# Low halves of the mixer's weights: a negated copy on ScalarE and an accumulating DMA in place of VectorE's subtraction

## The chip, the core and the metric

The kernel runs on one core of a Trainium2 chip. The metric is the device time of one execution in microseconds: 2360.43 us is the median of three runs, which lie between 2358.93 and 2362.97 us.

## The reference

Two transformer-like blocks follow each other on 1024 tokens of width 1024, all in float32. What matters here is the first block's input projection and its two branches:

```python
h = rms_norm(x, g_mix[l])
z = jnp.einsum("bsd,de->bse", h, w_in[l]) + b_in[l]
va, ga, xb, gb, sa, sb = jnp.split(z, cuts, axis=-1)
u = va * jax.nn.sigmoid(ga)
u = causal_depthwise_conv(u, conv_a_w[l], conv_a_b[l])
...
v = causal_depthwise_conv(xb, conv_b_w[l], conv_b_b[l])
v = rg_lru(v, w_rg_a[l], b_rg_a[l], w_rg_x[l], b_rg_x[l], lam[l])
y_b = jnp.einsum("bsc,cd->bsd", v * jax.nn.gelu(gb), w_b_out[l])
m = jax.nn.sigmoid(sa) * y_a + jax.nn.sigmoid(sb) * y_b
```

`w_in` has 7168 columns, `rg_lru` holds two small matrices per head (16 heads of width 96) and a scan over time. An output projection, an MLP and the whole second block come after; the change does not touch their code.

## The kernel before, in words

Activations lie transposed: channels on the 128 partitions, tokens along the row, in two halves of 512 tokens. To keep float32 precision every operand of a matrix product is split into a high part in fp32r and the low part that is left, and a product is three matmuls: low by high, high by low, high by high. A weight unit is a tile of 128 by 1024: eight input chunks of one block of 128 output channels. One product of a unit with one half of the tokens (`ct`, L134) is therefore 24 matmuls of 512 columns, 16 on L124 and 8 on L127, into one PSUM bank; four banks (`pm`) rotate.

`weight` (L102 to L111) makes a unit ready: SP issues the load of 512 KB into a staging tile `wst` (L106; two such tiles), ScalarE copies it into the high part `wh` in fp32r (L108), and VectorE subtracts that from the staging tile into the low part `wl` (L110). There are four tiles each of `wh` and `wl` (`N_W`, L1241), so a new unit's copy waits until PE is done with an older one. The three instructions run under a raised priority (`W_AHEAD`), which places them ahead of the program's order in each engine's queue; each queue then runs in order.

`mixer_in` (L508) makes four rounds. A round r first runs `branch_b_in` (L370) for three units of the recurrent branch: two products, bias on ScalarE (L376), a first tap on ScalarE (L381), three taps on VectorE (L383), a split (L131, L132). Then comes the filler: in the rounds 0 to 2 `branch_a_pair` (L312), whose four units all stay loaded while the first half of the tokens passes and then the second; in round 3 two `sig_chunk`s. Then the gates: one unit `w_rg` (L399), and for each of four heads (n = 0 to 3) four small products, and a chain on ScalarE of sigmoid (L417), exp (L422), tanh (L426), square (L429), then VectorE (L430), then square root (L433); for n below 3 also a unit of the gelu gate (L437), two products and the gelu on ScalarE (L443, L444). VectorE multiplies and scans (L456 to L460). At the end of a round some `sig_chunk`s (L467): two products and a sigmoid on ScalarE (L473). The 31 taps of the other branch (`conv_a`, L358 to L365) fill VectorE's queue throughout, at a lowered priority.

ScalarE needs another function table for each kind of function. A change of table shows in the trace as idle time of 1.31 us ahead of an instruction.

Of the kernel before, what the change touches and what calls it, by code (L numbers as in the profile page):

```python
# [9 lines left out]
F32 = mybir.dt.float32  # L10
F32R = mybir.dt.float32r
AF = mybir.ActivationFunctionType
ALU = mybir.AluOpType
# [35 lines left out]
class Act:  # L49
    def __init__(self, n):  # L50
        self.n = n
        self.h = {}
        self.l = {}
# [8 lines left out]
class Builder:  # L62
    def __init__(self, nc, tc, io, out):
        self.nc, self.tc, self.io, self.out = nc, tc, io, out
        self.n = 0
        self.log1p = set()

    def name(self, s):
        self.n += 1
        return f"{s}_{self.n}"  # L70
# [31 lines left out]
    def weight(self, src, cols=1024):  # L102
        nc = self.nc
        with self.tc.high_priority(offset=W_AHEAD):
            st = self.wst.tile([P, cols], F32, tag="wst", name=self.name("wst"))
            nc.sync.dma_start(st, src)  # L106
            h = self.wh.tile([P, cols], F32R, tag="wh", name=self.name("wh"))
            nc.scalar.activation(h, st, AF.Copy)  # L108
            l = self.wl.tile([P, cols], F32R, tag="wl", name=self.name("wl"))
            nc.vector.tensor_tensor(l, st, h.bitcast(F32), ALU.subtract)  # L110
        return h, l  # L111

    def mm3(self, ps, terms, ordered=False):
# [393 lines left out]

    def mixer_in(self):  # L508
        self.uc = {}
        n_s = (0, 2, 5, 7, 12)  # L510
        for r in range(4):
            if r == 0:
                self.sig_chunk(0, (0,), self.w_sig)
                for c in range(2):
                    self.uc[c] = self.page(f"e{c}")
                    self.conv_a(c, self.a_first[c][2], self.uc[c])
            sig = list(range(max(n_s[r], 1), n_s[r + 1]))
            self.branch_b(r, lambda: [self.branch_a_pair(2 * r + 2)] if r < 3 else [self.sig_chunk(c) for c in sig[:2]])
            for c in (sig[2:] if r == 3 else sig):
                self.sig_chunk(c)  # L520
        self.u = Act(KC)
        for hf in range(2):
            self.ln_stats(hf)
        ws = [self.sig_chunk(12 + i, (0,)) for i in range(4)]
        self.ln_apply(0)
        for i in range(4):
            self.sig_chunk(12 + i, (1,), ws[i])
        self.ln_apply(1)
# [832 lines left out]
```

## Time and profile before

| | |
|---|---|
| median of 3 runs | 2360.43 us |
| the profiled execution, its own time | 2360.36 us |
| its span, first to last instruction | 2358.7 us |
| PE busy | 2309.5 us (98%), 10488 matmuls |
| VectorE (DVE) busy | 1707.4 us (72%) |
| ScalarE (ACT) busy | 896.0 us (38%) |
| GpSimd (POOL) busy | 18.8 us (1%) |
| mean granted TensorE clock | 0.992 of full speed |
| DMA | 199.48 MB, mean 85 GB/s |

The shares are means over a kernel whose stages differ. The four rounds of `mixer_in` lie between about 46 and 640 us. A busy PE in these pages is one whose matmuls overlap each other: the rate is read better from the number of matmuls in a stretch than from its busy time.

### The profile page before, as it was taken

The numbers are of one execution on the slowest core, as the hardware profiler recorded it, in microseconds if no ns is written. First come the engines' busy times: TensorE is split into PE (matmuls) and PEld (weight loads), VectorE is DVE, ScalarE is ACT, GpSimd is POOL, SyncE is SP. The second block draws the span as 40 slices with busy tenths as digits, with TensorE's granted clock in tenths as the row PEclk, the third lists the DMA queues.
The fourth block names the chain that finished last, engine by engine and source line by source line (L and its number), as shares of the span: only waits on it lengthen the run. The fifth ranks groups of instructions, "written<-read, shape, count | busy, mean of one in ns | idle before, by whom it ended". The sixth has DMA issues, their size and how long they took to land. (4 is left out here: it accounts for less than half of the span.)

```text
span 2358.7 us, 27111 instructions
## 1 busy us (share of the span) xinstructions
PE 2309.5 (98%) x10488; PEld 1903.8 (81%) x10488; DVE 1707.4 (72%) x2567; ACT 896.0 (38%) x1372; POOL 18.8 (1%) x44
## 2 busy tenths in 40 slices
PE   8999999999999999999999999999799999999998
PEld 6887888878878888888888888887687888888777
DVE  8999999895674334686676767678957467775866
ACT  6445463555552112342212212124624344443422
POOL 0000000000000000000000000000000000000000
PEclk9999999999999999999999999999899999999999
DMA  4223223233424323251211111111332111223422
GB/s 157 81 65 98 70 80 104 78 104 94 150 81 155 105 85 99 76 183 45 63 45 54 46 55 52 54 54 52 112 109 66 55 50 57 83 65 106 139 85 72
DMA packets 81090, 199.48 MB, mean 85 GB/s; under 512 B 9776, under 2 KB 12336, under 8 KB 80960
## 3 DMA queue, kind: packets, MB, share of 16 engines
q1 hardware_dynamic: 80960, 197.75, 26.5%
q8 instruction: 82, 1.34, 0.2%
q14 instruction: 48, 0.39, 0.1%
HBM read 157.83 MB, written 38.31 MB: 83 GB/s over the span
## 5 line engine op out<-in xcount | busy, mean ns | idle before, releaser
L124 PE MATMUL pm<-acth,wl 128*128 128x512 f32 (+1 forms) x2032 | 786.6, 389 | 9.9 <-ACT b L473 5.0
L124 PE MATMUL pm<-actl,wh 128*128 128x512 f32 (+1 forms) x2032 | 787.7, 389 | 0.4 <-DVE actl L132 0.4
L127 PE MATMUL pm<-acth,wh 128*128 128x512 f32 (+1 forms) x2032 | 510.2, 387 | 0.0
L124 PEld LDWEIGHTS pm<-acth,wl 128*128 128x128 f32 x2032 | 383.4, 189 | 89.7 <-ACT b L473 6.3
L124 PEld LDWEIGHTS pm<-actl,wh 128*128 128x128 f32 x2032 | 383.5, 189 | 79.7 <-DVE actl L132 2.4
L127 PEld LDWEIGHTS pm<-acth,wh 128*128 128x128 f32 x2032 | 377.6, 188 | 76.1 <-issue 0.7
L108 ACT ACTIVATE wh<-wst 128x1024 fp32r<-128x1024 f32 x181 | 190.7, 1056 | 336.8 <-PE pm L127 238.1
L110 DVE TENSOR_TENSOR wl<-wst,wh 128x1024 fp32r<-128x1024 f32 x181 | 220.7, 1222 | 110.5 <-ACT wh L108 109.6
L807 DVE TENSOR_TENSOR x<-pm,x 128x512 f32<-128x512 f32 x240 | 161.2, 689 | 66.4 <-PE pm L127 51.7
L124 PE MATMUL pm<-e,wh 128*128 128x512 f32 x480 | 186.9, 389 | 0.0
L124 PE MATMUL pm<-e,wl 128*128 128x512 f32 x480 | 178.5, 390 | 0.0
L668 ACT ACTIVATE wh<-wst 128x1024 fp32r<-128x1024 f32 (+1 forms) x56 | 53.4, 954 | 260.6 <-PE pm L127 225.1
L127 PE MATMUL pm<-e,wh 128*128 128x512 f32 x480 | 141.8, 390 | 0.0
L358 DVE SCALAR_TENSOR_TENSOR e<-roll,pv,e 128x507 f32<-128x507 f32 (+14 forms) x174 | 119.9, 741 | 0.0
L124 PEld LDWEIGHTS pm<-e,wh 128*128 128x128 f32 x480 | 90.2, 188 | 18.9
L127 PEld LDWEIGHTS pm<-e,wh 128*128 128x128 f32 x480 | 90.1, 188 | 18.9
L124 PEld LDWEIGHTS pm<-e,wl 128*128 128x128 f32 x480 | 90.3, 188 | 18.4
L692 PE MATMUL pa<-acth,wl 128*128 128x512 f32 x224 | 87.3, 390 | 0.0
L692 PE MATMUL pa<-actl,wh 128*128 128x512 f32 x224 | 87.3, 390 | 0.0
L119 PE MATMUL pm<-e,wh 128*128 128x512 f32 x256 | 80.4, 399 | 0.6 <-DVE e L275 0.6
L131 ACT ACTIVATE e<-b 128x512 fp32r<-128x512 f32 x64 | 40.3, 632 | 103.1 <-DVE b L799 97.6
L702 DVE TENSOR_TENSOR b<-b,pa 128x512 f32<-128x512 f32 x70 | 46.8, 685 | 37.1 <-PE pa L692 36.0
(365 smaller groups left out, 3181.8 us busy)
## 6 DMA issues: line engine op xcount, KB each, us to landing
wst<-in_w_in SPq DMA_DIRECT2D x89, 512.0 KB, 3.5
wst<-in_w SPq DMA_DIRECT2D x64, 512.0 KB, 3.5
sig<-b SPq DMA_DIRECT2D x32, 256.0 KB, 2.7
ld<-sig SPq DMA_DIRECT2D x32, 256.0 KB, 2.6
a<-p SPq DMA_DIRECT2D x24, 256.0 KB, 3.7
wst<-in_w_b_out SPq DMA_DIRECT2D x12, 512.0 KB, 4.6
y<-b SPq DMA_DIRECT2D x24, 256.0 KB, 2.3
wst<-in_w_out SPq DMA_DIRECT2D x12, 512.0 KB, 3.5
```

What stands on the lines that cost most here:

```text
L108: nc.scalar.activation(h, st, AF.Copy)
L110: nc.vector.tensor_tensor(l, st, h.bitcast(F32), ALU.subtract)
L119: self.nc.tensor.matmul(ps, a, b, start=i == 0, stop=i == n - 1)
L124: self.nc.tensor.matmul(ps, a, b, start=i == 0, stop=i == n - 1)
L127: self.nc.tensor.matmul(ps, aH, bH, start=i == 0, stop=i == n - 1)
L131: self.nc.scalar.activation(H, srcap, AF.Copy)
L358: ops.append(lambda k=k: V.scalar_tensor_tensor(out[:, k:], x[:, :HALF - k], taps[k], out[:, k:], ALU.mult, ALU.add))
L668: nc.scalar.activation(h[:, :n], src, AF.Copy)
L692: self.nc.tensor.matmul(ps, (aH, aL)[i], (bH, bL)[j], start=n == 0, stop=n == 11)
L702: V.tensor_tensor(out, a, b, op)
L807: self.nc.vector.tensor_tensor(x, ps, x, ALU.add)
```

## The change

A flag `low_by_dma` is set while the four rounds of `mixer_in` are built and cleared before the layer norm. In a unit made under it the subtraction on VectorE is not issued. ScalarE writes the negated high part into `wl` right behind its copy, and GpSimd issues a DMA that reads the unit from DRAM a second time and adds it onto `wl`. All else is as before.

```diff
@@ class Builder, __init__ @@
         self.log1p = set()
+        self.low_by_dma = False
@@ weight @@
             nc.scalar.activation(h, st, AF.Copy)
             l = self.wl.tile([P, cols], F32R, tag="wl", name=self.name("wl"))
-            nc.vector.tensor_tensor(l, st, h.bitcast(F32), ALU.subtract)
+            if self.low_by_dma:
+                nc.scalar.activation(l, h.bitcast(F32), AF.Copy, scale=-1.0)
+                nc.gpsimd.dma_start(l, src, accum_op=ALU.add)
+            else:
+                nc.vector.tensor_tensor(l, st, h.bitcast(F32), ALU.subtract)
         return h, l
@@ mixer_in @@
         self.uc = {}
+        self.low_by_dma = True
         n_s = (0, 2, 5, 7, 12)
         for r in range(4):
...
         self.u = Act(KC)
+        self.low_by_dma = False
         for hf in range(2):
             self.ln_stats(hf)
```

## Rows read from the trace of the kernel before

**Rows 1.** Windows: us, PE, PEld, DVE, ACT, POOL busy (count), PE clock, DMA, GB/s.

```profile
59.00:118.00 59.00, 59.00 (x262) 48.87 (x261) 58.99 (x79) 26.05 (x34) 0.00 (x0) 1.00 0.26 81
177.00:236.00 59.00, 56.49 (x242) 46.22 (x241) 59.00 (x82) 32.64 (x49) 0.00 (x0) 0.97 0.33 98
472.00:531.00 59.00, 56.47 (x242) 46.27 (x241) 56.95 (x79) 31.95 (x46) 0.00 (x0) 0.97 0.33 104
```

**Rows 2.** Waits of PE, 0 to 720 us: us in total, times, longest.

```profile
PE pm L119 <- ACT e L274: 8.2, 1, 8.2
PE pm L124 <- ACT b L473: 5.0, 2, 2.5
PE pm L124 <- DVE x L553: 0.8, 1, 0.8
```

**Rows 3.** Timeline of PE, the first long wait in round 0.

```profile
212.16 0.50 PE L124 MATMUL pm<-acth,wl 128*128 128x512 f32 x1 [2.51 <-ACT b L473]
```

**Rows 4.** Timeline of ACT, round 0: start us, us, instruction, [idle before <-releaser].

```profile
160.36 1.06 ACT L108 ACTIVATE wh<-wst 128x1024 fp32r<-128x1024 f32 x1
...
164.60 1.29 ACT L417 ACTIVATE a<-pa,pv 96x512 f32<-96x512 f32 x2 [1.76 <-DVE a L457]
...
174.25 1.04 ACT L108 ACTIVATE wh<-wst 128x1024 fp32r<-128x1024 f32 x1
...
206.60 1.05 ACT L108 ACTIVATE wh<-wst 128x1024 fp32r<-128x1024 f32 x1
208.96 1.15 ACT L433 ACTIVATE a<-a 96x512 f32<-96x512 f32 x2 [1.31 <-DVE a L430]
211.42 0.69 ACT L473 ACTIVATE b<-pm,pv 128x512 f32<-128x512 f32 x1 [1.31 <-issue]
```

**Rows 5.** Windows of L110 alone (DVE), then of L108 alone (ACT): busy (count), PE clock, DMA, GB/s.

```profile
46.00:604.00 558.00, 62.28 (x51) 0.99 0.28 86
...
46.00:604.00 558.00, 53.87 (x51) 0.99 0.28 86
```

**Rows 6.** Timeline of DVE behind the copy at 160.36.

```profile
161.46 1.23 DVE L110 TENSOR_TENSOR wl<-wst,wh 128x1024 fp32r<-128x1024 f32 x1
162.60 1.28 DVE L456 TENSOR_TENSOR a<-a,c 96x512 f32<-96x512 f32 x2
```

**Rows 7.** Timelines of ACT and PE, rounds 1 and 3: sigmoid that frees a bank, and its taker.

```profile
344.18 0.69 ACT L473 ACTIVATE b<-pm,pv 128x512 f32<-128x512 f32 x1 [1.31 <-issue]
344.92 0.50 PE L124 MATMUL pm<-acth,wl 128*128 128x512 f32 x1
...
349.59 1.27 ACT L473 ACTIVATE b<-pm,pv 128x512 f32<-128x512 f32 x2 [1.31 <-issue]
350.49 0.39 PE L124 MATMUL pm<-acth,wl 128*128 128x512 f32 x1
...
619.18 0.69 ACT L473 ACTIVATE b<-pm,pv 128x512 f32<-128x512 f32 x1 [1.31 <-issue]
621.90 0.39 PE L124 MATMUL pm<-acth,wl 128*128 128x512 f32 x1
```

**Rows 8.** Window around the wait of 0.8 us on L553.

```profile
685.00:690.00 5.00, 4.22 (x19) 3.12 (x18) 1.82 (x2) 3.69 (x7) 0.00 (x0) 1.00 0.25 57
```

**Rows 9.** Line L106 from 46 to 640 us: issue of a unit's load to its landing.

```profile
DMA to landing us min/median/max: 3.4/3.5/5.4
```

**Rows 10.** ACT's copy of the last unit of each pair, and PE's first use.

```profile
100.68 1.07 ACT L108 ACTIVATE wh<-wst 128x1024 fp32r<-128x1024 f32 x1 [0.34 <-PE pm L127]
111.36 0.39 PE L124 MATMUL pm<-acth,wl 128*128 128x512 f32 x1
...
236.88 1.04 ACT L108 ACTIVATE wh<-wst 128x1024 fp32r<-128x1024 f32 x1
246.58 0.39 PE L124 MATMUL pm<-acth,wl 128*128 128x512 f32 x1
...
392.75 1.05 ACT L108 ACTIVATE wh<-wst 128x1024 fp32r<-128x1024 f32 x1
399.45 0.39 PE L124 MATMUL pm<-acth,wl 128*128 128x512 f32 x1
```

## The prediction

> **What bounds the kernel now.** I read the windows by stage first. In the rounds of `mixer_in` VectorE looks like the bound: 58.99 of 59 us. But PE is full as well, and it is PE that sets the pace: 262 matmuls in 59 us is one in 0.225 us, and no slice does better. Two slices fall short, with 242 matmuls and a mean clock of 0.97 [rows 1]. Each lacks 20 matmuls, 20 x 0.225 = 4.5 us. So the view to read next is PE's waits: up to 720 us there are only 8.2 us at the start, ahead of the change, two waits of 2.5 us for the sigmoid on L473, and 0.8 us on L553 [rows 2]. In each short slice 2.5 us of the 4.5 are the wait; the other 2.0 are the lower clock behind it. VectorE releases nothing that PE waits for in the rounds: its full queue is mostly filler, the 31 taps.
>
> Why is the sigmoid late? PE has run four products ahead, so all four banks are full, and it stands until ScalarE frees the first [rows 3]. The timeline of ScalarE shows why: from the gates of head 1 on, copies, table changes and gate functions follow without another gap, and the idle times are the 1.31 us of a table. At 206.60 comes a weight copy, at 208.96 the square root, at 211.42 the sigmoid [rows 4]. **In the heads' loop ScalarE, not VectorE, is late**, and the change moves work onto it.
>
> **The change part by part.**
>
> *VectorE loses 51 subtractions*, 62.28 us [rows 5]. Credit by itself: 0, since PE never waits for them [rows 2]; the cover is that units are ready early, and even the latest low part, behind the copy at 392.75, is there at about 395.3 for a first use at 399.45 [rows 10]. Without that cover each would cost its 1.22 us. One spot counts. At 161.46 a subtraction stands ahead of the products L456, and ScalarE's gates at 164.60 wait for that chain [rows 4, 6]. Without it the chain starts up to 1.2 us earlier. I take 1.2 in rounds 0 to 2, where VectorE is full; the other end is 0.
>
> *ScalarE gains 51 negated copies.* The nearest row is its own copy of the same tile, 53.87 / 51 = 1.06 us [rows 5], so 54 us in all. A copy needs no new wait and has the same priority, so I place it right behind the first copy. Most lie in ScalarE's pauses and cost nothing. In the heads' loop four copies precede the late sigmoid: 160.36, where the wait of 1.76 us takes it in, 174.25, 206.60 [rows 4] and one of the same kind between them. The sigmoid moves by 3 x 1.06 - 1.2 = 2.0 us.
> - Round 0 and round 2 (same order, PE wait already there): +2.0 us each.
> - Round 1 has no wait today, but no reserve either: the sigmoid at 344.18 ends 0.05 us before PE takes its bank at 344.92. So +2.0. The next sigmoid, of the pair at 349.59, ends at 350.22 against 350.49, a reserve of 0.27, and one more copy stands ahead of it: +0.8 [rows 7]. Of the clock: after waits of 2.5 us it fell, around the 0.8 us of L553 it stayed at 1.00 [rows 2, 8]; 2.0 is nearer to 2.5, so +2.0.
> - Round 3: the sigmoid ends at 619.87 and the bank is taken at 621.90, a reserve of 2.0 [rows 7]; two copies take it up, 0.
>
> Sum for ScalarE: 2.0 + 4.8 + 2.0 = 8.8 us. Ends: 0, if the copies are placed elsewhere; without VectorE's 1.2 it is 12.4, and with a third copy in round 3 (3 x 1.06 - 2.0) 1.2 more, 13.6.
>
> *GpSimd gains 51 accumulating DMAs.* It is idle here [rows 1], so nothing is queued behind its wait for the negation. No row shows such a DMA. Below: the plain load of the same 512 KB lands after 3.4 to 5.4 us, 3.5 in the median [rows 9]. It has to read two operands, so I take 2 x 3.5 = 7.0 us, issue included, and twice the longest, 10.8, as the upper end; 3.5 is the lower. DMA engines are busy 28% here [rows 5]; 51 units read twice add about as much again, and that fits.
>
> By the Trainium skill, DMA: Bandwidth & Descriptors, section on the anatomy of a DMA on the GpSimd path, one takes 2.0 us and its bytes at 436 GB/s; Collectives: The Full Stack, section on the bandwidth ceiling, has an adding DMA read two sources through the same ring, at half rate. An estimate from both is 2.0 + 2 x 1.2 = 4.4 us; the rows have nothing to test it, and with it the next term would be 0 and the sum 2369.2.
>
> Who waits for the low part? PE's first matmul of a unit uses it. The dangerous unit is the last of each pair, whose tile comes free only two products before it is used. The negation follows the copy, whose successor starts some 0.96 us after it:
> - round 0: 101.64 + 1.06 + 7.0 = 109.7 against 111.36: 0.
> - round 1: 237.83 + 1.06 + 7.0 = 245.9 against 246.58: 0.
> - round 2: the copy is late, at 392.75; 393.70 + 1.06 + 7.0 = 401.8 against 399.45: 2.3 us, and 2.0 of clock: +4.3 [rows 10].
>
> At 10.8 us the three are 2.1, 3.1 and 6.1 us with 2.0 each: 17.3.
>
> *The staging tile* comes free after ScalarE's copy instead of VectorE's subtraction, so SP loads earlier by one to three us; loads are not what the units wait for: 0. What SP has queued behind them moves earlier too. With the cover gone, a load costs its 3.5 us [rows 9].
>
> **Sum**: 8.8 + 4.3 = 13.1 us. The profiled execution took 2360.36 us, span 2358.7 and 1.7 around it, and lies on the median of 2360.43. 2360.4 + 13.1 = **2373.5 us**, 0.55% slower.
>
> **The rivals.**
> - *Faster: VectorE's relief frees the heads' loop.* Subtractions stand in the queue among L430, L456 to L460, and ScalarE waits for these in turn; if each round's chain shortens by more than the 3.2 us of three negations, the sigmoids are in time and both long waits go with their clock: 2360.4 - 2 x 4.5 = 2351.4. For it: VectorE is full, and the wait of 1.76 us on L457 [rows 4]. Against it: behind it ScalarE's only idle time is that of tables, 1.31 us each [rows 4]. Chance 0.15.
> - *No change*: the scheduler puts negations into ScalarE's pauses, or relief and load cancel (8.8 falls to about 0), and the DMA lands within 5 us: 2360 to 2362. For it: ScalarE is busy for only some 30 of 59 us [rows 1]. Against it: the raised priority. Chance 0.20.
> - *Much slower: the accumulating DMA takes 10.8 us or more.* From about 8.7 us on, round 0 waits as well. 8.8 + 17.3 = 26.1, 2386.5. For it: nothing in this trace shows an adding DMA. Against it: the engines have room. Chance 0.15. The Trainium skill, SBUF — State Buffer, section on SBUF's two separate sides, in its note on "The 'DVE blocks DMA' trap", says that a DMA issued from GpSimd starves while VectorE runs in a mode that takes both shared ports; it would bring this case about. Its section on who interferes with whom excepts `tensor_tensor` from these modes, and VectorE runs mostly operations with two inputs here; no run here shows either.
> - *The change does less than it says*: the flag covers 51 units, counted above, and no other; units of the layer norm and later keep VectorE. I see no way that it misses those 51, so this has no chance of its own.
>
> **How the numbers follow.** The forecast has 0.50: with a range of its own from 2365 to 2378. A measurement of this kernel can tell about 0.2%, 4.7 us, from no change. Slower: 0.50 + 0.15 = 0.65; same 0.20; faster 0.15. The range: from 2355, which holds no change and a part of faster, to 2387, which holds the long DMA; terms at both upper ends, 13.6 + 17.3, would give 2391 and are left out, as is the heart of the faster case.
>
> **What would show it.** 51 ScalarE instructions of about 1.06 us, no L110 from 46 to 604 us, and 51 issues on GpSimd whose landing is near 7.0 us. PE's wait for L473 in rounds 0 and 2 at about 4.5 us, a new one in round 1 at 2 us or more. A wait of PE for a low part's DMA near 400 us, none in rounds 0 and 1. VectorE some 60 us less busy, and PE's count in its full slices still 262. The prediction is wrong if the sigmoids come no later than before, which makes the relief of VectorE the larger effect, or if DMA waits show at many units, which makes the landing the one cost that counts.

## The result and the profile after

The changed kernel takes 2379.91 us (median of four executions, 2376.9 to 2382.4). Beside it on the same chip the kernel before took 2361.7 (2358.93 to 2363.12). The ratio is 1.0084, with a 95% interval of 1.0071 to 1.0096: slower by 0.8%. The profiled execution took 2378.24 us, span 2376.3, so 17.6 us of span are to be found.

In the changed file the lines stand some lines lower: L109 is ScalarE's copy (L108 before), L112 its negated copy, L113 the DMA of GpSimd, L422 the gates' sigmoid (L417), L438 the square root (L433), L449 the gelu (L444), L461 and L462 VectorE's products (L456, L457), L478 the late sigmoid (L473), L363 the taps (L358), L129 the matmuls of L124.

First the page's busy times. The change did what it says: VectorE lost 53.9 us (1707.4 to 1653.5), ScalarE gained 47.1 (896.0 to 943.1).

```profile
PE 2314.9 (97%) x10488; PEld 1906.6 (80%) x10488; DVE 1653.5 (70%) x2516; ACT 943.1 (40%) x1423; POOL 63.1 (3%) x95
```

The line of the negated copies and, from the line of GpSimd's DMAs, issue to landing:

```profile
L112 ACT ACTIVATE wl<-wh x51: 1039/1049/1068, 48.1 to 624.0; 128x1024 fp32r<-128x1024 f32 x51
```

```profile
L113 POOL DMA_DIRECT2D wl<-in_w_in x47: 853/867/1013, 49.4 to 625.4; - x47
...
DMA to landing us min/median/max: 5.2/5.7/9.2
```

PE's waits up to 720 us answer to [rows 2]:

```profile
PE pm L129 <- ACT b L478: 13.9, 3, 5.5
PE pm L124 <- ACT e L279: 9.4, 2, 8.4
PE pa L129 <- ACT a L422: 2.1, 3, 0.7
...
PE pm L129 <- DMA wl<-in_w_in: 0.3, 1, 0.3
```

The wait for the sigmoid has grown from 5.0 to 13.9 us and from two to three times, new ones of 2.1 us are for the gates' banks (`pa`), and PE waits 0.3 us in all for the new DMAs. Where they lie, the timeline of PE tells (start, length, instruction, idle before and what ended it):

```profile
216.31 0.80 PE L129 MATMUL pm<-acth,wl 128*128 128x512 f32 x1 [5.47 <-ACT b L478]
...
252.14 0.47 PE L129 MATMUL pm<-acth,wl 128*128 128x512 f32 x1 [0.31 <-DMA wl<-in_w_in]
...
354.53 0.50 PE L129 MATMUL pm<-acth,wl 128*128 128x512 f32 x1 [2.99 <-ACT b L478]
...
515.44 0.79 PE L129 MATMUL pm<-acth,wl 128*128 128x512 f32 x1 [5.43 <-ACT b L478]
```

One long wait for each of the rounds 0 to 2. The windows (columns as in [rows 1]) price them, lower clock included, by the matmuls that a slice lacks. The slices of round 1 in the kernel before:

```profile
236.00:295.00 59.00, 59.00 (x262) 48.80 (x261) 59.00 (x85) 26.82 (x38) 0.00 (x0) 1.00 0.23 70
295.00:354.00 59.00, 58.95 (x260) 48.39 (x259) 58.92 (x87) 36.71 (x56) 0.00 (x0) 1.00 0.27 81
354.00:413.00 59.00, 59.00 (x262) 48.87 (x261) 55.06 (x72) 18.90 (x23) 0.00 (x0) 1.00 0.33 103
```

and the changed kernel:

```profile
177.00:236.00 59.00, 52.90 (x221) 42.95 (x220) 58.97 (x89) 39.82 (x56) 5.20 (x6) 0.94 0.57 143
236.00:295.00 59.00, 58.69 (x259) 48.25 (x258) 47.20 (x66) 26.50 (x36) 4.38 (x5) 1.00 0.50 114
295.00:354.00 59.00, 55.81 (x245) 45.45 (x243) 48.16 (x74) 38.84 (x59) 3.48 (x4) 1.00 0.51 116
354.00:413.00 59.00, 58.47 (x251) 48.22 (x252) 43.87 (x56) 30.07 (x37) 5.22 (x6) 0.97 0.66 167
...
472.00:531.00 59.00, 52.83 (x225) 42.90 (x224) 44.11 (x67) 37.69 (x56) 4.35 (x5) 0.94 0.56 138
```

Round 0 does 221 where the kernel before did 242 [rows 1]: 21 x 0.225 = 4.7 us. Round 2: 225 for 242, 3.8 us. In round 1 the three slices did 262, 260 and 262 before; they lack 3 + 15 + 11 = 29, 6.5 us. That is 15.0 of the 17.6 us. The start adds little: the waits for L279 grew there from 8.2 to 9.4 us, but up to 59 us PE has done 204 matmuls for 206, 2 x 0.225 = 0.45 us. The rest, some 2 us, comes after 1670 us, far behind the change: the matmul that starts at 1670 us in the kernel before starts 15.3 us later here, the last one 17.6.

Why the sigmoid is later is seen in ScalarE's timeline of round 0, which answers to [rows 4]:

```profile
151.10 1.05 ACT L112 ACTIVATE wl<-wh 128x1024 fp32r<-128x1024 f32 x1
...
161.65 1.06 ACT L109 ACTIVATE wh<-wst 128x1024 fp32r<-128x1024 f32 x1
162.74 1.06 ACT L112 ACTIVATE wl<-wh 128x1024 fp32r<-128x1024 f32 x1
165.59 1.29 ACT L422 ACTIVATE a<-pa,pv 96x512 f32<-96x512 f32 x2 [1.79 <-DVE a L462]
...
175.27 1.04 ACT L109 ACTIVATE wh<-wst 128x1024 fp32r<-128x1024 f32 x1
...
182.92 1.06 ACT L112 ACTIVATE wl<-wh 128x1024 fp32r<-128x1024 f32 x1
185.30 2.41 ACT L422 ACTIVATE a<-pa,pv 96x512 f32<-96x512 f32 x4 [1.31 <-DVE b L465]
...
200.19 1.06 ACT L112 ACTIVATE wl<-wh 128x1024 fp32r<-128x1024 f32 x1
202.57 2.41 ACT L422 ACTIVATE a<-pa,pv 96x512 f32<-96x512 f32 x4 [1.31 <-DVE e L363]
...
212.16 1.15 ACT L438 ACTIVATE a<-a 96x512 f32<-96x512 f32 x2 [1.31 <-DVE a L435]
213.21 1.04 ACT L112 ACTIVATE wl<-wh 128x1024 fp32r<-128x1024 f32 x1
215.57 0.69 ACT L478 ACTIVATE b<-pm,pv 128x512 f32<-128x512 f32 x1 [1.31 <-issue]
```

The sigmoid starts at 215.57 for 211.42: 4.15 us later. Three negations, at 182.92, 200.19 and 213.21, stand between the gates of head 1 and the sigmoid, where the chain has no idle time but the 1.31 us of a table: 49.98 us from gates to sigmoid for 46.82, 3.16 us. The other 0.99 is there when the gates start (165.59 for 164.60); 0.29 of it is older than the loop's negations, for the last of head 0's gates already starts at 147.87 for 147.58. The negation at 162.74 costs nothing itself, since the gates wait behind it for VectorE's L462 anyway; it is that product which comes later. On ScalarE the negation at 151.10, in head 0, has moved the square root ahead of the products by 1.2 us (156.34 for 155.10).

Why the freed subtraction did not bring the products forward is seen on VectorE. The kernel before, ahead of the rows of [rows 6]:

```profile
158.03 3.34 DVE L358 SCALAR_TENSOR_TENSOR e<-e,pv,e 128x503 f32<-128x503 f32 x5
```

and the changed kernel:

```profile
159.02 4.67 DVE L363 SCALAR_TENSOR_TENSOR e<-e,pv,e 128x503 f32<-128x503 f32 x7
163.61 1.29 DVE L461 TENSOR_TENSOR a<-a,c 96x512 f32<-96x512 f32 x2
```

Five taps and a subtraction took 3.34 + 1.23 us; now seven taps take 4.67. Two more filler taps stand in the place of the subtraction, the stretch begins 1.0 us later than before, and so do the products (163.61 for 162.60).

### The profile page after: what moved, and what is told of

It reads as the page before. It is cut to its first block, busy times and chain, and to the rows that moved or that the text cites. A ratio compares the mean times of both kernels' runs of the same rounds, so it can differ in the third digit from the quotient of the medians.

```text
span 2376.3 us, 27244 instructions
## 1 busy us (share of the span) xinstructions
PE 2314.9 (97%) x10488; PEld 1906.6 (80%) x10488; DVE 1653.5 (70%) x2516; ACT 943.1 (40%) x1423; POOL 63.1 (3%) x95
## 5 line engine op out<-in xcount | busy, mean ns | idle before, releaser
L129 PE MATMUL pm<-acth,wl 128*128 128x512 f32 (+1 forms) x2032 | 788.5, 389 | 19.0 <-ACT b L478 13.9
L129 PE MATMUL pm<-actl,wh 128*128 128x512 f32 (+1 forms) x2032 | 788.7, 389 | 0.4 <-DVE actl L137 0.4
L129 PEld LDWEIGHTS pm<-acth,wl 128*128 128x128 f32 x2032 | 384.8, 189 | 99.8 <-ACT b L478 15.2
L129 PEld LDWEIGHTS pm<-actl,wh 128*128 128x128 f32 x2032 | 384.8, 189 | 79.6 <-DVE actl L137 1.7
L109 ACT ACTIVATE wh<-wst 128x1024 fp32r<-128x1024 f32 x181 | 190.5, 1056 | 346.4 <-PE pm L132 243.8
L115 DVE TENSOR_TENSOR wl<-wst,wh 128x1024 fp32r<-128x1024 f32 x130 | 158.3, 1221 | 88.3 <-ACT wh L109 87.7
L129 PE MATMUL pm<-e,wh 128*128 128x512 f32 x480 | 186.8, 389 | 0.0
L129 PE MATMUL pm<-e,wl 128*128 128x512 f32 x480 | 178.4, 390 | 0.0
L363 DVE SCALAR_TENSOR_TENSOR e<-roll,pv,e 128x510 f32<-128x510 f32 (+14 forms) x174 | 117.4, 736 | 2.1 <-ACT e L360 2.0
L129 PEld LDWEIGHTS pm<-e,wh 128*128 128x128 f32 x480 | 90.1, 188 | 18.8
L129 PEld LDWEIGHTS pm<-e,wl 128*128 128x128 f32 x480 | 90.1, 188 | 18.3
L124 PE MATMUL pm<-e,wh 128*128 128x512 f32 x256 | 80.1, 397 | 0.5 <-DVE e L280 0.5
```

Source lines behind the costliest of these rows:

```text
L124: self.nc.tensor.matmul(ps, a, b, start=i == 0, stop=i == n - 1)
L129: self.nc.tensor.matmul(ps, a, b, start=i == 0, stop=i == n - 1)
L363: ops.append(lambda k=k: V.scalar_tensor_tensor(out[:, k:], x[:, :HALF - k], taps[k], out[:, k:], ALU.mult, ALU.add))
```

## The experiments

Theory A: the negated copies in ScalarE's chain in the heads' loop are the price. Its rivals: the adding DMA is the price, by its landing or its traffic (B); the relief of VectorE is worth something, so that the true price is larger (C); every unit has the same price, wherever it lies (D). Diffs are against the changed kernel unless another is named; the kernel before ran beside each batch (2359.66, 2358.88, 2359.63 and 2358.82 us).

### The negated copies alone

```diff
-                nc.gpsimd.dma_start(l, src, accum_op=ALU.add)
```

> The 51 low tiles hold only ScalarE's negated copy; the accumulating DMA is left out, so their low parts are wrong and the second read of the weights is missing. Theory A (the negated copies lengthen ScalarE's chain in the heads' loop, the DMA is hidden): as the changed kernel, 2376 to 2382 us, with PE waiting 12 to 15 us for the sigmoid. Theory B (the DMA from GpSimd and its second read cost the time): about 2361 us, waits for the sigmoid near 5 us.

This kernel leaves out the addition, so its low parts hold no weights; only its time counts here. Measured: 2373.54 us (2372.56 to 2374.93), ratio 1.006 [1.0043, 1.0077], a little below what A asked. PE's waits for ScalarE are those of the changed kernel (L477 and L421 are its L478 and L422):

```profile
PE pm L128 <- ACT b L477: 13.9, 3, 5.5
...
PE pa L128 <- ACT a L421: 2.1, 3, 0.7
```

So 13.9 us of the loss (2373.54 - 2359.66) need no DMA at all.

### The DMA alone

```diff
-                nc.scalar.activation(l, h.bitcast(F32), AF.Copy, scale=-1.0)
-                nc.gpsimd.dma_start(l, src, accum_op=ALU.add)
+                nc.gpsimd.dma_start(l, src)
```

> The 51 low tiles are loaded from DRAM by a plain DMA from GpSimd; the negation and the subtraction are both left out, so the low parts hold whole weights. Theory A: ScalarE's chain is as before, 2357 to 2363 us, PE's waits for the sigmoid near 5 us. Theory B: 2374 to 2382 us. Theory C (VectorE's relief is worth something that ScalarE's loss hides): below 2356 us, the waits for the sigmoid shorter than 5 us.

This kernel leaves out the negation, so its low parts hold whole weights. Measured: 2362.31 us (2357.64 to 2363.73), ratio 1.001 [1.0001, 1.002]. The waits for the sigmoid are in sum where they were, 5.0 before (one has grown from 2.5 to 3.4 us, the other shrunk to 1.8):

```profile
PE pm L128 <- ACT b L477: 5.2, 2, 3.4
```

VectorE is as free here as in the changed kernel, ScalarE does no more than before, and nothing is gained: C finds no support. The second read from DRAM, with landings of 3.9 us in the median, comes with a loss of 2.7 us (2362.31 - 2359.66). VectorE relieved without any DMA was not run, so a relief worth as much as that DMA costs is not excluded; the waits show none.

### The negation kept, the addition on VectorE

```diff
-                nc.gpsimd.dma_start(l, src, accum_op=ALU.add)
+                nc.vector.tensor_tensor(l, st, l.bitcast(F32), ALU.add)
```

> ScalarE writes the negated copy as in the change, but VectorE adds the staged weight onto it; no DMA from GpSimd, VectorE is not relieved. Theory A: 2376 to 2384 us, as the changed kernel or a few us more. Theory B: 2359 to 2364 us. Theory C: above the changed kernel by what the relief is worth, over 2384 us.

Measured: 2377.21 us (2376.36 to 2379.87), ratio 1.0077 [1.0062, 1.0092]. The waits for the sigmoid come to 13.6 us, for the gates' banks to 4.5. Without the DMA and without any relief the time is nearly that of the change. Against the negations alone, VectorE's 51 additions cost 3.7 us, 2.4 of them as waits for the gates' banks. So by this pair the relief is worth some 4 us once ScalarE's chain is the longer one, and the change has that already.

### The negation on GpSimd

```diff
-                nc.scalar.activation(l, h.bitcast(F32), AF.Copy, scale=-1.0)
+                nc.gpsimd.tensor_scalar(l, h.bitcast(F32), -1.0, None, ALU.mult)
```

> The negation is made by GpSimd instead of ScalarE, the accumulating DMA follows it on the same queue. Theory A: the sigmoid is as early as before, 2357 to 2364 us, unless GpSimd's negation takes over 4 us, when low parts of the last unit of each pair come late and PE waits for their DMA. Theory B: 2374 to 2384 us. Theory C: below 2356 us.

Measured: 2387.97 us (2386.17 to 2388.25), ratio 1.0119 [1.0104, 1.0134], the slowest of all. The line of the negation:

```profile
L112 POOL TENSOR_SCALAR wl<-wh x51: 2760/3114/12592, 47.8 to 626.3; 128x1024 fp32r<-128x1024 f32 x51
```

and PE's waits up to 740 us:

```profile
PE pm L129 <- DMA wl<-in_w_in: 11.6, 3, 5.3
PE pm L129 <- ACT b L478: 8.6, 3, 4.3
```

A negation of 4.15 us in the mean (211.3 us for 51) makes the low parts late, and PE waits at 114.45, 260.85 and 422.46, where it first uses the last unit of each pair, the units of [rows 10]. The path that the prediction named is real: with negations 3.1 us longer than ScalarE's it is the largest wait. PE also waits 8.6 us for the sigmoid, 5.0 before, though ScalarE does no negation here. VectorE is slower beside the busy GpSimd (1683.9 us busy for 1653.5 in the changed kernel); whether that is the cause was not tried.

### Which units: pairs and gates, or the rest

The flag set ahead of the filler and cleared behind the gates' unit (18 units), and the reverse (33 units, those of the heads' loop among them):

```diff
 vs = [self.branch_b_in(3 * g + j, j, v_d) for j in range(3)]
+self.low_by_dma = True
 filler()
 w = self.weight(self.io["w_rg"][g])
+self.low_by_dma = False
```

> Negation on ScalarE and accumulating DMA only for the 18 units whose copies lie outside the heads' loop (the pairs of the other branch, the two sigmoid units in their place in round 3, the gates' unit w_rg); the other 33 keep VectorE's subtraction. Theory A (only negations inside ScalarE's closed chain cost): 2358 to 2363 us, PE's waits for the sigmoid 5 to 6 us. Theory D (every unit costs the same, wherever it lies): 18/51 of 18 us, about 2366 us.

> The complement: the change only for the 33 units of the recurrent branch's input, the gelu gates and the sigmoids, most of whose copies lie in the heads' loop; the other 18 keep VectorE. Theory A: nearly the whole loss, 2374 to 2381 us, waits for the sigmoid 12 to 15 us in three places. Theory D: 33/51 of 18 us, about 2372 us.

Measured: the 33 units 2374.37 us (2371.81 to 2374.86), ratio 1.0062 [1.0047, 1.0078], with the waits for the sigmoid at 13.9 us again, as A asks. The 18 units 2367.7 us (2367.0 to 2368.67), ratio 1.0038 [1.0024, 1.0051]: a miss for A, and nearer to the 2366 of D. Its timeline shows where half of the 8.8 us go. ScalarE, then PE:

```profile
393.82 1.05 ACT L109 ACTIVATE wh<-wst 128x1024 fp32r<-128x1024 f32 x1
394.77 0.68 ACT L381 ACTIVATE x<-pm,pv 128x512 f32<-128x512 f32 x1
395.34 1.05 ACT L112 ACTIVATE wl<-wh 128x1024 fp32r<-128x1024 f32 x1
```

```profile
404.38 0.47 PE L129 MATMUL pm<-acth,wl 128*128 128x512 f32 x1 [2.61 <-DMA wl<-in_w_in]
```

GpSimd issues the DMA at 396.80, it lands 7.5 us later, and PE has stood for 2.61 us. The window of that stretch has 242 matmuls at a clock of 0.97, where the kernel before did 262: 20 x 0.225 = 4.5 us. This is the prediction's term for round 2, which the changed kernel itself does not show: there round 1 has already made PE some 11 us late, the copy comes at 400.00, the DMA is issued at 402.98 and lands in 5.4 us, before PE needs it. Another 14 matmuls, 3.2 us, are missing from 295 to 354 us (246 for 260), where PE waits 1.80 us for the gates' banks and 0.99 for the sigmoid although no negation stands in that loop; the cause of these stays open. D has its own test below, where the negations stay and only the sigmoid moves.

### The high part on GpSimd instead

Against the kernel before, for all 51 units (the flag set as in the change) and for the 33 (the flag as in the second of the two above):

```diff
-            nc.scalar.activation(h, st, AF.Copy)
+            if self.low_by_dma:
+                nc.gpsimd.tensor_copy(h, st)
+            else:
+                nc.scalar.activation(h, st, AF.Copy)
```

> The opposite of the change: VectorE's subtraction stays as before, and ScalarE is rid of its copy into the high part too, which GpSimd makes for the same 51 units; no DMA from GpSimd. Theory A: ScalarE's chain is 3 to 4 us shorter per round, so both waits of 2.5 us with their slow clock go: 2350 to 2357 us, unless GpSimd's copy is over 5 us or slows VectorE so that units or gates come late. Theory C (VectorE's load matters): slower than before, over 2364 us.

> As the run before, but GpSimd makes the high part only for the 33 units of the recurrent branch's input, the gelu gates and the sigmoids; the units of the pairs and w_rg keep ScalarE's copy. Theory A: 2350 to 2356 us, as the run before or a little better, since only copies in the heads' loop count. Theory C: slower than before, over 2362 us.

Measured: 2382.38 us (2381.76 to 2383.94), ratio 1.0101 [1.0087, 1.0114], and 2373.54 (2370.5 to 2374.53), ratio 1.006 [1.0047, 1.0072]. Both miss what A asked and lie where C put them: ScalarE is relieved of these copies, and the kernel is slower. The line of GpSimd's copy and PE's waits, 51 units:

```profile
L110 POOL CAST wh<-wst x51: 1038/1595/9628, 46.4 to 621.1; 128x1024 fp32r<-128x1024 f32 x51
```

```profile
PE pa L128 <- ACT a L421: 9.0, 5, 4.6
...
PE pm L128 <- ACT b L477: 7.1, 3, 2.5
```

PE now waits for the gates, and the gates for VectorE: it is busy 1734.7 us for 1707.4 before, its taps have a mean of 777 ns for 741, and its products L460 start at 172.00 behind taps, so that ScalarE's gates stand for 3.60 us at 174.01. So VectorE is not free of price: ScalarE's chain runs through it, and these gates stand behind a VectorE that is busy some 27 us longer. How much of the loss is the slower VectorE and how much another order of its queue stays open, and these two runs say nothing of what ScalarE's relief alone is worth.

### The sigmoid earlier

If the wait for the sigmoid is the price, moving the sigmoid out of the chain removes it. In each round the two sigmoids of the first `sig_chunk` behind the loop go right behind the gates' sigmoids of the last head, which use the same function, under a raised priority (`urgent`); first in the kernel before, then in the changed one:

```diff
+            self.last_gate = sig
...
-            nc.scalar.activation(t, ps, AF.Sigmoid, bias=self.vec("b_in", 40 + c))
+            with self.urgent() if early else nullcontext(), self.after(self.last_gate if early else None):
+                nc.scalar.activation(t, ps, AF.Sigmoid, bias=self.vec("b_in", 40 + c))
...
+            for i, c in enumerate(sig[2:] if r == 3 else sig):
+                self.sig_chunk(c, early=i == 0)
```

> The kernel before, with one thing moved: the two sigmoids of the first sigmoid unit of each round run right behind the fourth head's gate sigmoids, in the same table, instead of behind that head's square root. Theory A (the lateness of this sigmoid on ScalarE is what PE waits for): both waits of 2.5 us and their slow clock go, 2 x 4.5 us, 2349 to 2354 us. Otherwise 2358 to 2363 us.

> The changed kernel with the same move of the sigmoids. Theory A: the bank is free some 4 us before PE asks for it even with the negations, so the three waits (13.9 us) and their slow clock go and only the waits for the gates' banks (2.1 us) and the like are left: 2352 to 2360 us, at most 8 us above the early sigmoid without the change. Theory D (each unit's negation or DMA costs wherever it lies): 15 us or more above it, over 2366 us.

Measured: the kernel before with this, 2355.73 us (2353.83 to 2358.76), ratio 0.9984 [0.9975, 0.9993]; the changed kernel with this, 2357.89 (2356.09 to 2360.51), ratio 0.9992 [0.9983, 1.0001]. The first on ScalarE:

```profile
199.58 2.41 ACT L417 ACTIVATE a<-pa,pv 96x512 f32<-96x512 f32 x4 [1.31 <-DVE b L461]
201.88 1.26 ACT L475 ACTIVATE b<-pm,pv 128x512 f32<-128x512 f32 x2
```

and in windows:

```profile
177.00:236.00 59.00, 59.00 (x262) 48.82 (x261) 59.00 (x82) 33.71 (x49) 0.00 (x0) 1.00 0.34 99
295.00:354.00 59.00, 56.17 (x233) 45.51 (x232) 59.00 (x87) 36.52 (x56) 0.00 (x0) 0.94 0.33 97
472.00:531.00 59.00, 59.00 (x262) 48.83 (x261) 57.07 (x79) 32.56 (x47) 0.00 (x0) 1.00 0.35 107
```

The short slices of rounds 0 and 2 are full, 2 x 4.5 us won. But round 1 lost 27 matmuls, 6.1 us, to a new wait of 2.56 us on the gates' banks (319.21) and the clock behind it, so the gain falls short of what was expected. Why those gates come late was not followed. In the changed kernel the same move takes away 20 to 22 us, more than the change had cost, and leaves these waits up to 740 us:

```profile
PE pm L129 <- DMA wl<-in_w_in: 3.4, 2, 1.9
PE pa L129 <- ACT a L422: 2.1, 3, 0.8
```

No wait for a sigmoid is left, and with it goes nearly the whole price of the change, 51 negations and 51 DMAs notwithstanding: that is A, and D, which asked for over 2366 us, falls. What is left, 2.2 us between the two, is a balance: the waits for low parts, of 1.54 us at 223.44 and 1.90 at 401.14, stand against the wait of 2.56 us at 319.21, which only the other of the two has. The kernel before with the early sigmoid is faster than both kernels compared here, by 0.16% against the kernel before; the interval just leaves out 1.

### The changed kernel again, and with a DMA that overwrites

```diff
-                nc.gpsimd.dma_start(l, src, accum_op=ALU.add)
+                nc.gpsimd.dma_start(l, src)
```

> The changed kernel itself, beside the next kernel and beside the kernel before on one chip: between the run with the negated copies alone (2373.5) and the first runs of the changed kernel (2379.9) 6.4 us are unexplained, of which the profile shows 0.3 as a wait for a low part and 1.0 at the start. If the adding DMA has a price of that size, this stays at 2378 to 2382 against some 2360 for the kernel before. If the gap is mostly the difference between chips and executions, it comes out at 2374 to 2377.

> As the changed kernel, but the DMA of GpSimd overwrites the low part with the weights in place of adding to it (so the low part is the whole unit, and the output is not the reference's). ScalarE's negations, GpSimd's waits and issues and the second read from DRAM all stay; only the addition is gone. If only ScalarE's negations count, this lies within 2 us of the changed kernel of the same batch, with the same three waits for the sigmoid (13.9 us) and no wait for a low part, landings near 3.9 us. If the addition's longer landing or its reading of the tile costs something, it lies 3 to 6 us below the changed kernel, at 2373 to 2376.

The second kernel leaves out the addition, so its low parts hold whole weights. Measured in one batch: the changed kernel 2378.31 us (2377.3 to 2380.73), ratio 1.0085 [1.0071, 1.0099]; with the overwriting DMA 2376.0 (2375.54 to 2378.23), ratio 1.0076 [1.0063, 1.009]. Both have the 13.9 us for the sigmoid. The changed kernel waits 0.9 us for a low part, the other nowhere. The landings of the overwriting DMA:

```profile
DMA to landing us min/median/max: 3.7/4.5/6.3
```

Taken against the kernel before of each batch, the loss is 19.5 us (2378.31 - 2358.82) for the change and 13.9 for the negations alone. So the DMAs beside the negations seem to cost some 5.6 us; their runs do not overlap, but the intervals of the two ratios do ([1.0071, 1.0099] and [1.0043, 1.0077]). The overwriting DMA lies between the two cases that were expected of it: by the medians 3.3 of the 5.6 us go to a DMA of GpSimd and 2.3 to its addition, which is no more than the 2 to 4 us by which the runs of one kernel spread. The windows up to 590 us, the negations alone, with the overwriting DMA, the change:

```profile
0.00:590.00 590.00, 564.91 (x2444) 463.56 (x2445) 485.03 (x734) 338.87 (x472) 0.91 (x9) 0.99 0.29 91
```

```profile
0.00:590.00 590.00, 563.45 (x2440) 462.69 (x2441) 485.36 (x734) 339.00 (x472) 26.50 (x57) 0.99 0.44 133
```

```profile
0.00:590.00 590.00, 563.79 (x2430) 462.29 (x2431) 482.88 (x732) 336.90 (x471) 42.82 (x57) 0.98 0.54 133
```

The overwriting DMA lacks 4 matmuls there, 0.9 us; the rest of its 3.3 was not found. The addition lacks 10 more, 2.3 us. Of these 0.9 us are the wait for the low part. Most of the others lie from 354 to 413 us, behind a sigmoid's wait as long in both (2.99 and 2.97 us): 245 matmuls at a clock of 0.94 against 253 at 0.97. That the addition has to do with this clock is not shown.

## Why the prediction was right, and where its sum was not

The forecast was 2373.5 us and slower; it came out slower by the first of the two mechanisms that the prediction added up, and 6.4 us later. By its steps:

- **What bounds the kernel**: right. In the rounds PE stands for ScalarE's sigmoid, and VectorE's full queue does not set the time. The DMA alone, with VectorE relieved, gains nothing.
- **VectorE's subtractions at 0**: right by the DMA alone; with the negations in place the relief is worth some 4 us. The 1.2 us of relief counted in rounds 0 to 2 is the step that failed. In round 0, where it was followed, two filler taps took the place of the subtraction at 161.46, and the products came 1.0 us later, not 1.2 earlier [rows 6].
- **ScalarE's term, 8.8 us**: right in mechanism, too small. "Three negations less 1.2" gave 2.0 us a round; it was three negations, 3.16 us, and gates that themselves started 0.99 later: 0.29 from the start of the kernel and 0.70 behind a fourth negation in head 0, which the prediction had not counted. So 4.15 us on the sigmoid in round 0. That the fourth negation is the cause of the 0.70 was not tried alone, but other runs agree. From the last gate of head 0 to the first of head 1 the kernel before takes 17.02 us, the changed one 17.72 and the one with the negations alone 17.71; with the 18 units and with the DMA alone, which have no negation there, it is 17.04 and 16.90. That the negations stand behind the gelus and the square root and not right behind their copies changed nothing, for the chain has no pause between these places. Not foreseen at all were the waits of 0.6 to 0.7 us for the gates' banks, which wait for the same chain. By rounds, clock included: 4.7, 6.5 and 3.8 us for 2.0, 4.8 and 2.0; round 3 at 0 was right (262 matmuls from 531 to 590 us for 261). In round 1 a wait of 2.99 us stands where 2.0 + 0.8 were expected.
- **The accumulating DMA, 4.3 us**: landing 5.7 us in the median for the 7.0 taken, between the bounds of 3.5 and 10.8. In the changed kernel the term was nearly empty, 0.31 us, and that lay in round 1, at 252.14, where none was expected and the DMA took 7.3 us to land. In round 2 the rounds ahead had already moved PE away from the landing. Where PE is late by some 2 us only, with the 18 units alone, it was there at about the size written: a wait of 2.61 us for 2.3, and 4.5 us with its clock for 4.3, by a landing of 7.5. Two terms had been added that hide each other, and this offset two thirds of what the ScalarE term lacked (4.0 of 14.7 - 8.8 = 5.9 us). That the sum came as near as 6.4 us is in this part luck.
- **The staging tile, 0**: no wait for a load shows in PE's waits. The 0.45 us at the start, and some 2 us behind 1670 us, had no term.

By the estimate from the Trainium skill (DMA: Bandwidth & Descriptors, section on the anatomy of a DMA on the GpSimd path, with Collectives: The Full Stack, section on the bandwidth ceiling) the landing would have been 4.4 us. The trace has 5.2 us as the shortest and 5.7 in the median, so the measurement decides; the median lies midway between that estimate and the 7.0 taken.

Of the rivals, **faster** fell with the DMA alone: without any negation the freed VectorE leaves the sigmoid's waits at 5.2 us. **No change** asked for two things; the landing was nearly short enough, but the negations do stand in the chain. **Much slower** asked for 10.8 us, and the longest landing is 9.2. The starvation that the Trainium skill describes (SBUF — State Buffer, note on the "DVE blocks DMA" trap) does not show: GpSimd's issues last 853 to 1013 ns beside a full VectorE. Whether VectorE was ever in the mode that the Trainium skill names there, no run here shows.

## What to carry to other kernels

An engine's busy share does not say where an instruction is free: ScalarE was busy for 30 of 59 us and VectorE for all, yet taking 51 subtractions from VectorE did not bring the sigmoid forward, and a microsecond put into ScalarE's gapless chain of gates was paid in full, with the lower clock on top. Before moving work off a full engine, look whether its queue holds filler, which takes the freed place, and follow the chain that the late wait hangs on back to its last pause, counting every instruction that the change puts there. When costs add up along one path, ask whether the first already covers the next.

## What was not expected of the hardware

- **GpSimd beside a busy VectorE.** The same copy of 128x1024 took GpSimd between 1.04 and 9.63 us, the negation between 2.76 and 12.59, while the taps went from 741 to 777 and 784 ns. The Trainium skill (SBUF — State Buffer, section on who interferes with whom) has a VectorE instruction with two inputs in SBUF contend with a GpSimd instruction that reads SBUF; the trace agrees: while VectorE stood idle the copy took 1.04 us (at 438.14) and the negation 2.76 (at 281.1 and 441.9). The larger part falls on GpSimd. With the copies on GpSimd VectorE was busy 27 us longer in all, and the 51 copies took 133.9 us (152.7 - 18.8), 81 more than 51 of 1.04 us would, an estimate.
- **An adding DMA of 512 KB** from DRAM lands in 5.7 us, an overwriting one from GpSimd in 3.9 us in the kernel with the DMA alone and 4.5 behind the negations, the plain load by SP in 3.5 [rows 9]. Where the DMA engines were full (0.9 and more from 224 to 232, 364 to 372 and 522 to 530 us) the adding one took up to 7.9, 8.8 and 9.2. Its issue held GpSimd for 853 to 1013 ns, that of the overwriting one for 527 to 720.
- **The clock's price varies.** Waits of 2.5 us left a mean clock of 0.97 in the slice and 242 matmuls in the kernel before [rows 1]. In the kernel with the 18 units a wait of 2.56 us at 212.91 left 1.00 and 249, so that 13 matmuls were lost for 20. Waits of 5.4 to 5.5 us left 0.94 in the changed kernel, and 0.97 in that with the negations alone (472 to 531 us), with the same 225 matmuls. A price for the clock read off one wait is good to some 2 us only.
